# The up-projection of the ConvGatedMLP as a timed plan for four engines

## The chip, the cores and the metric

The kernel runs on one core of a Trainium2 chip. Five engines with queues of their own work side by side: TensorE (PE; its weight loads are PEld), VectorE (DVE), ScalarE (ACT), GpSimd (POOL) and SyncE (SP), which here issues the DMAs. Each engine works through its own instructions strictly in order and waits on semaphores for the others. The metric is the device time of one execution in microseconds (us), as the median of the runs shown.

## The reference

One decoder layer, sequence 1024, width 1024, all in float32: two gated token mixers, then the gated MLP with a causal convolution over three positions, then a gated per-layer embedding, each followed by a layer norm. The part that matters is the MLP's first half, with D_FF = 2816:

```python
h = causal_dwconv(x @ w_up[i], conv_w[i], conv_b[i])     # w_up: 1024 x 5632, three taps per channel
h_gate, h_val = jnp.split(h, 2, axis=-1)
ffn = (jax.nn.silu(h_gate) * h_val) @ w_down[i]
```

## The kernel before

The stages run one after the other: projections and mixers up to 1296 us, the up-projection from 1296 to 1736 us, the down-projection from there, then the embedding. All products are made from float32 operands split into a high part (`wh`, written by ScalarE, L101) and a low part (`wl` = operand minus high part, L106), so that one product is three matmuls (L155): high by high, high by low, low by high.

The up-projection computes x @ w_up in 22 **column pairs** f. A pair is 128 gate columns (block f) and 128 value columns (block 22 + f) for all 1024 positions. It is done as one step of a seven-product scheme for 2 by 2 blocks: the weights of the pair are four blocks 11, 12 (from the gate columns) and 21, 22 (from the value columns), which lie in two raw tiles of 512 KB (`wr` for even f, `ar` for odd f). Four **combinations** are formed in place in these tiles (L164 on VectorE, `wr<-wr,wr` or `ar<-ar,ar`): 11 - 21, 21 + 22, 22 - 11, 12 - 22. Seven operands, numbered j = 0 to 6, are split from the blocks before and after them. A combination overwrites what an earlier low part still reads, so it waits for that low part.

The steps of a pair, with the names used below:

- **products** p0 to p6: twelve matmuls each (4 slices of depth, 3 matmuls), `ch<-xs,wh` and `ch<-xs,wl`, into PSUM banks A to D (`ch`). There are 84 matmuls in a pair. In the order of the program p6 of a pair comes after p1 of the next.
- **sums** (L1043, VectorE, one operand in PSUM): five, which put the two halves of `h` together, and two **copies** on ScalarE (L1050, L1074).
- **convolution** of each half: a start on ScalarE (L1085), two **taps** on VectorE (L1087, both operands in SBUF), and for the gate half a **Silu** on ScalarE (L1089). The value half ("conv1") comes first, the gate half ("conv0") after p6.
- **gating product**: gate times value on GpSimd (L164, `cv<-cv,cv`, 128 x 1024), and its store to `d_act` by SP (L1097).

All seven low parts of a pair from the second on are made by GpSimd. Each operand has one pair of buffers, so the high part j of the next pair waits until product j of this one is done.

Inside this stage the order on each engine is set by the Tile scheduler, which takes the program's order (`up(f)` builds the steps, the loop at the end of the stage runs them) as priority and places every instruction by its own simulation of the engines. The program runs the steps of a pair as

```python
run([p0, p1, *late[:1], p5, *late[1:], p2, p3, p4, conv1])   # late = p6 and conv0 of the pair before
```

with the whole preparation of the pair's weights (`w_sets(f)`) ahead of it, and the gating product within `conv0`.

Of the kernel before, what the change touches and what calls it, by code (L numbers as in the profile page):

```python
# [17 lines left out]
P = 128  # L18
L = 1024
D = 1024  # L20
# [8 lines left out]
NF = FF // P  # L29
# [11 lines left out]
def hybrid_block(ctx: ExitStack, tc: tile.TileContext, x, p, w_in, w_gate_up, b_gate, g_gla, w_gla,  # L41
                 g_ckv, w_uv, w_dsa, w_out, ln1_g, ln1_b, w_up, conv_w, conv_b, w_down, ln2_g, ln2_b,
                 w_ple, w_ple_gate, ln3_g, ln3_b, out, tap=None):
    nc = tc.nc
    V, S, G, T = nc.vector, nc.scalar, nc.gpsimd, nc.tensor
    tap = tap or (lambda name, ap: None)
    x, p, out = x[0], p[0, 0], out[0]
# [13 lines left out]
    wq = pool("wparts", stack=sega)  # L61
# [8 lines left out]
    cw = cp.tile([P, 3, 2 * NF], F32, name="cw")  # L70
    cbias = cp.tile([P, 2 * NF], F32, name="cbias")
# [143 lines left out]
    def quad(a):  # L215
        return a.rearrange("p (a b) -> p a b", b=P)
# [39 lines left out]
    def run(steps):  # L256
        for f in steps:
            f()
# [16 lines left out]
    d_act = [dp.tile([P, 6, L], F32, name=f"d_act{c}") for c in range(4)]  # L275
# [47 lines left out]
    with ExitStack() as mix:  # L323
# [65 lines left out]
        with ExitStack() as c1:  # L389
# [15 lines left out]
            for t in range(NT):  # L405
                ps = bank("sm")
# [13 lines left out]
            for g in range(2):  # L420
                s = slice(g * HALF, (g + 1) * HALF)
# [6 lines left out]
            for j in range(4):  # L428
                un = wload(win_v, 0, KT, [(C_IQ + j * P, C_IQ + (j + 1) * P)], "A", "G")
                for g in range(2):  # L430
                    s = slice(g * HALF, (g + 1) * HALF)
                    ps = bank()
# [3 lines left out]
                                    op=ALU.subtract)  # L436
                    hi = xp.tile([P, HALF], F32R, name=nm("xh"), tag="xh", bufs=2)
# [3 lines left out]
                                    op=ALU.subtract)  # L441
# [3 lines left out]
            for g in range(2):  # L445
                s = slice(g * HALF, (g + 1) * HALF)
# [5 lines left out]
                for k in range(4):  # L452
# [4 lines left out]
                                op=ALU.subtract)  # L457
# [27 lines left out]
            raw = wp.tile([P, 1024], F32, name=nm("wr"), tag="wr", bufs=2)  # L485
# [197 lines left out]
        with ExitStack() as c3:  # L683
# [133 lines left out]
            plan = []  # L817
# [4 lines left out]
            for h in range(DH):  # L822
                b = 4 * h - 2.0 * h / (DH - 1)
# [174 lines left out]
    with ExitStack() as c1:  # L998
        psum_banks(c1, "d", ch=8)
        fp = pool("ffwork", stack=c1)  # L1000
        rawp = pool("raws", stack=segd, side="right")
        wk = pool("upwork", stack=segk, side="right")
        UE, UE0, US = 'GGGGGGG', 'VVGVVGV', 'VVVV'
        nset = [0]

        def blocks(f):

            return (NF + f, f) if f < NF - 1 else (f, NF + f)

        def w_sets(f):  # L1010
# [8 lines left out]
            W = []  # L1019
            for _ in range(7):  # L1020
                n = nset[0] % 7
                nset[0] += 1
                pl, nb = (wq, 4) if n < 4 else (fp, 3)
                W.append([pl.tile([P, 512], F32R, name=nm(x), tag=x, bufs=nb) for x in ("wh", "wl")])
            run(left_operands(raw[1][:, :512], raw[1][:, 512:], raw[0][:, :512], raw[0][:, 512:],
                              lambda j, src: split(*W[j], src, "A", (UE if f else UE0)[j]), US))
            return [[quad(t) for t in w] for w in W]

        def up(f):

            W = w_sets(f)
            st, out_ = {}, {}

            def prod(ps, j, start):
                for k in range(4):
                    mm3(ps, (W[j][0][:, k], W[j][1][:, k]), (XS[j][:, 0, k], XS[j][:, 1, k]), start and k == 0, k == 3,
                        not start)  # L1040

            def plus(out, a, b):
                V.tensor_tensor(out=out, in0=a, in1=quad(b), op=ALU.add)  # L1043

            def p0():
                st["A"] = bank("ch")
                prod(st["A"], 0, True)
                st["h"] = [wk.tile([P, L], F32, name=nm("h"), tag=f"h{i}", bufs=2) for i in range(2)]
                st["hv"] = [h.rearrange("p (a g q) -> p g a q", g=2, q=P) for h in st["h"]]
                S.activation(st["hv"][1][:, 0], quad(st["A"]), AF.Copy)  # L1050

            def p1():
                st["B"] = bank("ch")
                prod(st["B"], 1, True)
                plus(st["hv"][0][:, 1], st["hv"][1][:, 0], st["B"])

            def p5():
                st["C"] = bank("ch")
                prod(st["C"], 5, True)

            def p2():
                st["D"] = bank("ch")
                prod(st["D"], 2, True)

            def p3():
                prod(st["B"], 3, False)
                s1, u3 = st["hv"][1][:, 0], st["hv"][1][:, 1]
                plus(u3, s1, st["B"])
                plus(s1, u3, st["C"])
                plus(u3, u3, st["D"])  # L1070

            def p4():
                prod(st["A"], 4, False)
                S.activation(st["hv"][0][:, 0], quad(st["A"]), AF.Copy)  # L1074

            def p6():
                prod(st["D"], 6, False)
                o = st["hv"][0][:, 1]
                plus(o, o, st["D"])

            def conv(i):
                c = blocks(f)[1 - i]
                h = st["h"][i]
                o = out_[c // NF] = wk.tile([P, L], F32, name=nm("cv"), tag="cv", bufs=3)
                S.activation(o, h, AF.Identity, bias=cbias[:, c:c + 1], scale=cw[:, 2, c:c + 1])  # L1085
                for d in (1, 2):
                    V.scalar_tensor_tensor(o[:, d:], h[:, :L - d], cw[:, 2 - d, c:c + 1], o[:, d:], ALU.mult, ALU.add)  # L1087
                if c < NF:
                    S.activation(o, o, AF.Silu)  # L1089

            def conv1():
                conv(1)

            def conv0():
                conv(0)
                sums(out_[0], out_[0], out_[1], ALU.mult, "G")
                nc.sync.dma_start(d_act[f // 6][:, f % 6], out_[0])  # L1097
            return p0, p1, p5, p2, p3, p4, conv1, p6, conv0
# [18 lines left out]
    with ExitStack() as c1:  # L1117
# [251 lines left out]
```

## Time and profile before

| | us |
|---|---|
| median of 3 runs (2145.47 to 2150.24) | 2145.63 |
| profiled execution: its own time | 2145.27 |
| its span, first to last instruction | 2143.6 |
| TensorE matmul busy | 2063.3 (96%) |
| VectorE busy | 1564.6 (73%) |
| GpSimd busy | 1000.0 (47%) |
| ScalarE busy | 846.0 (39%) |
| mean granted TensorE clock | 0.984 |

The page says that TensorE is busy nearly all the time, but a matmul's busy time is its time in a pipeline, with neighbours overlapping: how fast the matmuls follow one another is read from the timeline, and how long they waited from the rows of a stretch.

### The profile page before, as it was taken

Reading aid. Unit: us, or ns where it says so; the run is one execution under the profiler, and the core shown is the slowest. Engines: PE = TensorE matmul, PEld = TensorE weight load, DVE = VectorE, ACT = ScalarE, POOL = GpSimd, SP = SyncE. Lnnn points to the kernel's source line nnn. Section 1 sums busy time; section 2 is a strip of 40 time slices with the busy share of each in tenths; the row PEclk is TensorE's granted clock in tenths of the full one; section 3 lists DMA queues with packets and bytes.
Section 4 is the critical chain, followed back from the end, with each engine's and each line's share of the span. In section 5 each row is a group of like instructions: output and inputs, shape, how many; then the busy total and the mean of one; then the engine's idle time right before and its main releaser. Section 6 shows DMA issues by size and latency. Waiting matters only on the chain.

```text
span 2143.6 us, 32563 instructions
## 1 busy us (share of the span) xinstructions
PE 2063.3 (96%) x12210; PEld 1811.3 (84%) x12210; DVE 1564.6 (73%) x2742; ACT 846.0 (39%) x1540; POOL 1000.0 (47%) x832
## 2 busy tenths in 40 slices
PE   9999999999999999999999978999999979999997
PEld 8888899998988888887788976877777769989897
DVE  3589999999227888876234487777777788895965
ACT  4343312213126766675222244344344353342421
POOL 2423444535422121213231586776776684554753
PEclk9999999999999999999999998999999989999999
DMA  4322211211226686779766442222222134323222
GB/s 138 79 64 79 86 31 57 57 50 52 64 86 130 130 157 130 144 158 212 205 216 122 147 153 87 86 72 87 81 69 89 64 109 148 118 94 119 89 99 79
DMA packets 377566, 227.14 MB, mean 106 GB/s; under 512 B 189328, under 2 KB 351760, under 8 KB 377408
## 3 DMA queue, kind: packets, MB, share of 16 engines
q1 hardware_dynamic: 377408, 225.06, 38.7%
q8 instruction: 96, 1.57, 0.3%
q14 instruction: 62, 0.51, 0.1%
HBM read 146.37 MB, written 40.89 MB: 87 GB/s over the span
## 4 chain that ended last, share of the span: by engine, by line
PE 29%; DVE 9%; POOL 7%; issue 5%; DMA 3%; ACT 2%; SPq 0%; POOLq 0%; DVEq 0%; ACTq 0%
PE ch L155 16%; PE mm L155 13%; POOL wl L106 4%; DVE cv L1087 1%; DMA wr<-d_ob 1%; DVE cx L164 1%; DMA dr<-in_w_down_dram 1%; DVE h L1043 1%; ACT cv L1085 1%; DVE ar L164 1%; DVE wu L106 1%; DVE res_all L910 1%; DVE res_all L164 0%; DVE stats L933 0%; POOL lnmv L212 0%
## 5 line engine op out<-in xcount | busy, mean ns | idle before, releaser
L106 POOL TENSOR_TENSOR wl<-wr,wh 128x512 fp32r<-128x512 f32 x304 | 439.8, 1461 | 288.3 <-ACT wh L101 280.7
L155 PE MATMUL ch<-xs,wh 128*128 128x512 f32 x1232 | 384.8, 394 | 5.8 <-ACT wh L101 3.2
L155 PE MATMUL mm<-Ah,wh 128*128 128x512 f32 x832 | 332.1, 399 | 2.7 <-ACT wh L101 1.6
L155 PE MATMUL mm<-Al,wh 128*128 128x512 f32 x832 | 330.4, 397 | 0.3 <-POOL Al L106 0.3
L155 PE MATMUL mm<-Ah,wl 128*128 128x512 f32 x832 | 329.4, 396 | 0.0
L155 PEld LDWEIGHTS ch<-xs,wh 128*128 128x128 f32 x1232 | 231.5, 189 | 58.7 <-DVE h L1043 4.1
L103 POOL TENSOR_SCALAR wh<-wr 128x512 fp32r<-128x512 f32 x112 | 75.2, 674 | 381.1 <-PE mm L155 194.4
L155 PE MATMUL ch<-xs,wl 128*128 128x512 f32 x616 | 242.8, 395 | 6.8 <-POOL wl L106 6.7
L155 PE MATMUL mm<-wl,Ah 128*128 128x256 f32 x768 | 217.1, 284 | 5.2 <-POOL wl L106 5.1
L155 PE MATMUL mm<-wh,Al 128*128 128x256 f32 x768 | 215.8, 283 | 0.0
L155 PE MATMUL ch<-wu,au 128*128 128x256 f32 x1512 | 194.0, 292 | 22.5 <-DVE au L106 7.2
L155 PE MATMUL mm<-wh,Ah 128*128 128x256 f32 x768 | 213.2, 283 | 0.0
L1087 DVE SCALAR_TENSOR_TENSOR cv<-h,cw,cv 128x1023 f32<-128x1023 f32 x88 | 168.6, 1915 | 60.0 <-ACT cv L1085 58.5
L155 PEld LDWEIGHTS ch<-wu,au 128*128 128x128 f32 x1512 | 190.4, 199 | 25.9 <-DVE au L106 8.1
L101 ACT ACTIVATE wh<-wr 128x512 fp32r<-128x512 f32 (+1 forms) x201 | 120.5, 623 | 194.7 <-PE mm L155 81.6
L155 PEld LDWEIGHTS mm<-Ah,wh 128*128 128x128 f32 x832 | 156.7, 188 | 33.4 <-ACT wh L101 2.1
L155 PEld LDWEIGHTS mm<-Ah,wl 128*128 128x128 f32 x832 | 156.4, 188 | 33.0
L155 PEld LDWEIGHTS mm<-Al,wh 128*128 128x128 f32 x832 | 156.5, 188 | 30.7 <-POOL Al L106 0.8
L674 DVE MATCH_REPLACE8 score<-m,score 128x896 f32<-128x896 f32 (+3 forms) x192 | 166.5, 869 | 0.0
L673 DVE MAX8 m<-score 128x8 f32<-128x896 f32 (+3 forms) x192 | 163.6, 876 | 2.3 <-POOL score L480 2.1
L155 PEld LDWEIGHTS mm<-wl,Ah 128*128 128x128 f32 x768 | 145.1, 189 | 7.1 <-POOL wl L106 6.4
L155 PEld LDWEIGHTS ch<-xs,wl 128*128 128x128 f32 x616 | 116.5, 189 | 38.2 <-POOL wl L106 14.0
(269 smaller groups left out, 4328.4 us busy)
## 6 DMA issues: line engine op xcount, KB each, us to landing
wr<-in_w_in_dram SPq DMA_DIRECT2D x60, 512.0 KB, 3.8
wr<-in_w_up_dram SPq DMA_DIRECT2D x22, 512.0 KB, 3.9
ar<-in_w_up_dram SPq DMA_DIRECT2D x22, 512.0 KB, 4.0
d_act<-cv SPq DMA_DIRECT2D x22, 512.0 KB, 2.6
dr<-in_w_down_dram SPq DMA_DIRECT2D x12, 768.0 KB, 7.0
ar<-d_act SPq DMA_DIRECT2D x12, 768.0 KB, 5.1
d_tg<-tg SPq DMA_DIRECT2D x32, 256.0 KB, 2.0
wr<-in_w_out_dram SPq DMA_DIRECT2D x16, 512.0 KB, 3.6
```

Source lines behind the costliest of these rows:

```text
L101: S.activation(dst, src, AF.Copy, scale=scale)
L103: (V if eng == "V" else G).tensor_scalar(dst, src, scale, 0.0, ALU.mult, ALU.add)
L106: done["GV"[eng != "G"]] = (G if eng == "G" else V).tensor_tensor(out=dst, in0=src, in1=hi.bitcast(F32), op=ALU.subtract)
L155: T.matmul(ps, lhsT=l, rhs=r, start=start, stop=stop, skip_group_check=more)
L164: (G if eng == "G" else V).tensor_tensor(out=out, in0=a, in1=b, op=op)
L673: V.max(m8, score[t])
L674: V.match_replace(score[t], m8, score[t], TAKEN)
L910: V.scalar_tensor_tensor(r[:, a:b], r[:, a:b], mv[:, 2:3], gb[1][:, a:b], ALU.mult, ALU.add)
L1043: V.tensor_tensor(out=out, in0=a, in1=quad(b), op=ALU.add)
L1085: S.activation(o, h, AF.Identity, bias=cbias[:, c:c + 1], scale=cw[:, 2, c:c + 1])
L1087: V.scalar_tensor_tensor(o[:, d:], h[:, :L - d], cw[:, 2 - d, c:c + 1], o[:, d:], ALU.mult, ALU.add)
```

## The change

`up` and `w_sets` go. In their place stand `plan_weights(f)` and `plan_pair(f)`, which give every operation of a pair a time: t0 = f * PAIR for products, sums, convolutions and store, and t0 = (f - 1) * PAIR for the weights, with PAIR = 7 * ON = 19.04 and ON = 2.72. The operations of all 22 pairs are sorted by this time and issued in that order inside `tc.manual_schedule` for TensorE, VectorE, ScalarE and GpSimd, so that these four keep it; SP is still placed by the scheduler. The times set an order and nothing else: no engine waits for a time. Which engine does an operation, its shape and its operands stay, and the seven low parts stay on GpSimd. The first pair's weights are prepared as before (`first_weights`), and the last pair's gate convolution and store run in the stage behind, as before.

```diff
-        def up(f):
-            W = w_sets(f)
...
-        late = []
         for f in range(NF):
-            p0, p1, p5, p2, p3, p4, conv1, *rest = up(f)
-            run([p0, p1, *late[:1], p5, *late[1:], p2, p3, p4, conv1])
-            late = rest
-        late[0]()
-        last_conv = late[1]
+            if f:
+                plan_weights(f)
+            last_conv = plan_pair(f)
+        with tc.manual_schedule(engines={nc.tensor.engine, nc.vector.engine, nc.scalar.engine, nc.gpsimd.engine}):
+            for _, _, step in sorted(plan, key=lambda e: e[:2]):
+                step()
...
+        def plan_weights(f):
+            t0 = (f - 1) * PAIR
...
+            def hi(t, j, src):
+                def f_():
+                    w[j] = w_place(j)
+                    hi_of(w[j][0], r[src], "A")
+                at_time(t0 + t, f_)
+            def lo(t, j, src):
+                at_time(t0 + t, lambda: lo_of(w[j][1], r[src], w[j][0], "G"))
+            def comb(t, out, x, y, op):
+                at_time(t0 + t, lambda: sums(r[out], r[x], r[y], op))
+            at_time(t0 - 8.0, load)
+            hi(3.3, 0, "11")
+            lo(3.9, 0, "11")
+            comb(6.1, "11", "11", "21", ALU.subtract)
...
+            def store():
+                sums(st["o", 0], st["o", 0], st["o", 1], ALU.mult, "G")
+                sent[0] = nc.sync.dma_start(d_act[f // 6][:, f % 6], st["o", 0])
...
+            last = conv(0, PAIR + 9.0, PAIR + 10.3, PAIR + 13.4) + [(t0 + 2 * PAIR + 5.5, store)]
...
-            last_conv()
+            run(last_conv)
```

What this does to the order shows in the middle of the stage. First GpSimd, from one column pair to the next. In the names `wr` and `ar` tell the pair whose weights are read, and the low parts follow one another as j = 1, 2, 3, 4, then 0 of the next pair. Before:

```order
L164 TENSOR_TENSOR cv_15130<-cv_15130,cv_15034 128x1024
L106 TENSOR_TENSOR wl_15189<-ar_15182,wh_15188 128x512
L106 TENSOR_TENSOR wl_15191<-ar_15182,wh_15190 128x512
L106 TENSOR_TENSOR wl_15193<-ar_15184,wh_15192 128x512
L106 TENSOR_TENSOR wl_15195<-ar_15184,wh_15194 128x512
L106 TENSOR_TENSOR wl_15331<-wr_15328,wh_15330 128x512
L106 TENSOR_TENSOR wl_15199<-ar_15184,wh_15198 128x512
L106 TENSOR_TENSOR wl_15341<-wr_15326,wh_15340 128x512
L164 TENSOR_TENSOR cv_15274<-cv_15274,cv_15178 128x1024
```

And now, with the low parts of j = 5, 1, 2, 3, 4 first:

```order
L106 TENSOR_TENSOR wl_15159<-ar_15017,wh_15158 128x512
L106 TENSOR_TENSOR wl_15182<-ar_15017,wh_15181 128x512
L106 TENSOR_TENSOR wl_15186<-ar_15017,wh_15185 128x512
L106 TENSOR_TENSOR wl_15203<-ar_15019,wh_15202 128x512
L106 TENSOR_TENSOR wl_15225<-ar_15019,wh_15224 128x512
L106 TENSOR_TENSOR wl_15246<-wr_15163,wh_15245 128x512
L164 TENSOR_TENSOR cv_15142<-cv_15142,cv_15064 128x1024
L106 TENSOR_TENSOR wl_15283<-ar_15019,wh_15282 128x512
L106 TENSOR_TENSOR wl_15303<-wr_15161,wh_15302 128x512
```

The gating product (L164) stood between the low parts of j = 5 and j = 1 and took the gate half whose Silu had just been made; now it stands between j = 0 of the next pair and j = 6, and belongs to a pair one earlier.

Second VectorE, over the same stretch: the last combination of a pair's weights, the first two of the next pair's, the sums (lines 1043 and 1111), the gate half's taps (lines 1087 and 1123) and the third combination. Before:

```order
L164 TENSOR_TENSOR ar_15184<-ar_15184,ar_15182 128x512
L164 TENSOR_TENSOR wr_15328<-wr_15328,wr_15326 128x512
L164 TENSOR_TENSOR wr_15326<-wr_15326 128x512
L1043 TENSOR_TENSOR h_15231<-h_15232,ch_15234 128x4x128
L1043 TENSOR_TENSOR h_15087<-h_15087,ch_15137 128x4x128
L1087 SCALAR_TENSOR_TENSOR cv_15274<-h_15087,cw,cv_15274 128x1023
L1087 SCALAR_TENSOR_TENSOR cv_15274<-h_15087,cw,cv_15274 128x1022
L164 TENSOR_TENSOR wr_15326<-wr_15326,wr_15328 128x512
```

And now:

```order
L164 TENSOR_TENSOR ar_15019<-ar_15019,ar_15017 128x512
L1111 TENSOR_TENSOR h_15262<-h_15243,ch_15230 128x4x128
L164 TENSOR_TENSOR wr_15163<-wr_15163,wr_15161 128x512
L164 TENSOR_TENSOR wr_15161<-wr_15161 128x512
L1111 TENSOR_TENSOR h_15118<-h_15118,ch_15145 128x4x128
L1123 SCALAR_TENSOR_TENSOR cv_15286<-h_15118,cw,cv_15286 128x1023
L1123 SCALAR_TENSOR_TENSOR cv_15286<-h_15118,cw,cv_15286 128x1022
L164 TENSOR_TENSOR wr_15161<-wr_15161,wr_15163 128x512
```

Only the sum behind p1 moved: it stands behind the first combination instead of behind the third.

Third TensorE, at the start of a pair, from the end of p0 (`xs_11727`) on; p1 reads `xs_11728`, p5 `xs_12438`, p6 of the pair before `xs_12439`. Before:

```order
L155 MATMUL ch_15362<-xs_11727,wh_15330 128x512 x2
L155 MATMUL ch_15362<-xs_11727,wl_15331 128x512
L155 MATMUL ch_15378<-xs_11728,wh_15332 128x512 x2
L155 MATMUL ch_15405<-xs_12438,wh_15340 128x512 x2
L155 MATMUL ch_15405<-xs_12438,wl_15341 128x512
L155 MATMUL ch_15405<-xs_12438,wh_15340 128x512
L155 MATMUL ch_15281<-xs_12439,wh_15198 128x512
L155 MATMUL ch_15378<-xs_11728,wl_15333 128x512
L155 MATMUL ch_15378<-xs_11728,wh_15332 128x512 x2
```

And now:

```order
L155 MATMUL ch_15354<-xs_11727,wh_15245 128x512 x2
L155 MATMUL ch_15354<-xs_11727,wl_15246 128x512
L155 MATMUL ch_15374<-xs_11728,wh_15325 128x512 x2
L155 MATMUL ch_15374<-xs_11728,wl_15326 128x512
L155 MATMUL ch_15374<-xs_11728,wh_15325 128x512 x2
L155 MATMUL ch_15374<-xs_11728,wl_15326 128x512
```

Before, six matmuls of p5 and p6 stood between the first two matmuls of p1 and the first that reads the low part of j = 1; now this one follows the first two directly, and p6 and p5 come after p1, each in one piece. On ScalarE the order within a pair is nearly the same; the start of the gate half's convolution stands ahead of the high part of j = 5, and the Silu ahead of that of j = 1, in both.

## Rows read from the trace of the kernel before

**Rows 1.** Busy time by stretch: stretch, length, engines (instructions), clock, DMA.

```profile
1322.50:1398.70 76.20, 76.20 (x338) 63.08 (x337) 57.06 (x52) 32.65 (x47) 51.44 (x29) 1.00 0.25 76
1398.70:1736.40 337.70, 330.90 (x1429) 265.29 (x1427) 245.55 (x220) 139.86 (x205) 237.59 (x136) 1.00 0.25 81
```

**Rows 2.** TensorE timeline: start, length, engine, line, operation, names, [idle before, releaser].

```profile
1559.52 0.50 PE L155 MATMUL ch<-xs,wl 128*128 128x512 f32 x1 [0.38 <-POOL wl L106]
...
1571.13 0.61 PE L155 MATMUL ch<-xs,wh 128*128 128x512 f32 x2
```

**Rows 3.** Waits 1296 to 1736: who waited for whom, us in total, times, longest.

```profile
PEld ch L155 <- POOL wl L106: 14.0, 17, 1.1
```

**Rows 4.** GpSimd timeline over one column pair.

```profile
1555.82 2.40 POOL L164 TENSOR_TENSOR cv<-cv,cv 128x1024 f32<-128x1024 f32 x1 [2.37 <-issue]
1558.19 6.99 POOL L106 TENSOR_TENSOR wl<-ar,wh 128x512 fp32r<-128x512 f32 x4
1565.14 1.28 POOL L106 TENSOR_TENSOR wl<-wr,wh 128x512 fp32r<-128x512 f32 x1
1567.78 1.67 POOL L106 TENSOR_TENSOR wl<-ar,wh 128x512 fp32r<-128x512 f32 x1 [1.35 <-ACT wh L101]
1571.52 1.82 POOL L106 TENSOR_TENSOR wl<-wr,wh 128x512 fp32r<-128x512 f32 x1 [2.06 <-ACT wh L101]
1575.70 2.42 POOL L164 TENSOR_TENSOR cv<-cv,cv 128x1024 f32<-128x1024 f32 x1 [2.37 <-issue]
```

**Rows 5.** VectorE timeline over the same column pair.

```profile
1558.49 4.29 DVE L1087 SCALAR_TENSOR_TENSOR cv<-h,cw,cv 128x1023 f32<-128x1023 f32 x2 [1.32 <-ACT cv L1085]
1565.21 1.76 DVE L164 TENSOR_TENSOR ar<-ar,ar 128x512 f32<-128x512 f32 x1 [2.43 <-POOL wl L106]
1566.90 0.68 DVE L164 TENSOR_TENSOR wr<-wr,wr 128x512 f32<-128x512 f32 x1
1567.61 0.69 DVE L164 TENSOR_TENSOR wr<-wr 128x512 f32<-128x512 f32 x1
1568.22 1.28 DVE L1043 TENSOR_TENSOR h<-h,ch 128x512 f32<-128x512 f32 x2
1570.90 3.52 DVE L1087 SCALAR_TENSOR_TENSOR cv<-h,cw,cv 128x1023 f32<-128x1023 f32 x2 [1.40 <-ACT cv L1085]
1574.34 0.68 DVE L164 TENSOR_TENSOR wr<-wr,wr 128x512 f32<-128x512 f32 x1
1574.94 2.12 DVE L1043 TENSOR_TENSOR h<-h,ch 128x512 f32<-128x512 f32 x3
```

**Rows 6.** ScalarE timeline, second half of the same pair.

```profile
1569.62 1.24 ACT L1085 ACTIVATE cv<-h,cbias,cw 128x1024 f32<-128x1024 f32 x1 [1.92 <-DVE h L1043]
1570.77 0.61 ACT L101 ACTIVATE wh<-wr 128x512 fp32r<-128x512 f32 x1
1574.51 1.06 ACT L1089 ACTIVATE cv<-cv 128x1024 f32<-128x1024 f32 x1 [3.12 <-DVE cv L1087]
1575.47 1.66 ACT L101 ACTIVATE wh<-wr 128x512 fp32r<-128x512 f32 x3
1577.09 1.25 ACT L1085 ACTIVATE cv<-h,cbias,cw 128x1024 f32<-128x1024 f32 x1
```

**Rows 7.** GpSimd timeline after the up-projection: its last gating product.

```profile
1767.08 2.70 POOL L164 TENSOR_TENSOR cv<-cv,cv 128x1024 f32<-128x1024 f32 x1
```

**Rows 8.** VectorE timeline beside that gating product.

```profile
1767.92 0.54 DVE L164 TENSOR_TENSOR ar<-ar,cx 128x384 f32<-128x384 f32 x1
...
1768.85 1.35 DVE L164 TENSOR_TENSOR dr<-dr 128x384 f32<-128x384 f32 x1
1770.12 0.55 DVE L164 TENSOR_TENSOR cx<-dr,cx 128x384 f32<-128x384 f32 x1
```

**Rows 9.** TensorE timeline at the start of the up-projection.

```profile
1304.27 2.69 PE L155 MATMUL ch<-xs,wh 128*128 128x512 f32 x5 [3.17 <-ACT wh L101]
```

**Rows 10.** Page, DMA issues: line, queue, count, KB each, us to landing.

```profile
wr<-in_w_up_dram SPq DMA_DIRECT2D x22, 512.0 KB, 3.9
```

More of the change, by code (lines that the diff above doesn't have):

```diff
@@ L1018, in w_sets @@
                 nc.sync.dma_start(raw[-1].rearrange("p (k c) -> p k c", k=KT), wup_v[:, :, c * P:(c + 1) * P])
[L1019 to L1026, printed above, removed]
@@ L1027, in w_sets @@
-            return [[quad(t) for t in w] for w in W]
-        def up(f):
-            W = w_sets(f)
[L1035 to L1081, printed above, removed]
@@ new lines, in raw_weights, with w_place, at_time, first_weights @@
+            return raw[1][:, :512], raw[1][:, 512:], raw[0][:, :512], raw[0][:, 512:]
+        def w_place(j):
+            pl, nb = (wq, 4) if j < 4 else (fp, 3)
+            return [pl.tile([P, 512], F32R, name=nm(x), tag=x, bufs=nb) for x in ("wh", "wl")]
+        plan = []
+        def at_time(t, f):
+            plan.append((t, len(plan), f))
+        W, ST, sent = {}, {}, [None]
+        def first_weights():
+            w = W[0] = {}
+            def put(j, src):
+                w[j] = w_place(j)
+                split(*w[j], src, "A", UE0[j])
+            run(left_operands(*raw_weights(0), put, US))
@@ new lines, in plan_weights, with load @@
+        def plan_weights(f):
+            w, r = {}, {}
+            t0 = (f - 1) * PAIR
+            W[f] = w
+            def load():
+                r.update(zip(("11", "12", "21", "22"), raw_weights(f)))
+            def hi(t, j, src):
+                def f_():
+                    w[j] = w_place(j)
+                    hi_of(w[j][0], r[src], "A")
[8 more added lines that the diff above has]
+            comb(6.1, "11", "11", "21", ALU.subtract)
+            comb(7.0, "21", "21", "22", ALU.add)
+            hi(11.0, 5, "22")
+            lo(11.6, 5, "22")
+            comb(13.3, "22", "22", "11", ALU.subtract)
+            hi(14.4, 1, "22")
+            lo(15.0, 1, "22")
+            hi(15.1, 2, "21")
+            lo(16.1, 2, "21")
+            hi(16.5, 3, "11")
+            lo(17.6, 3, "11")
+            hi(PAIR + 0.9, 4, "12")
+            lo(PAIR + 1.2, 4, "12")
+            comb(PAIR + 3.9, "12", "12", "22", ALU.subtract)
+            hi(PAIR + 8.3, 6, "12")
+            lo(PAIR + 8.9, 6, "12")
@@ new lines, in plan_pair, with prod, f_, half @@
+        def plan_pair(f):
+            t0 = f * PAIR
+            st = ST[f] = {}
+            def prod(n, ps, j):
+                def f_():
+                    start = ps not in st
+                    if start:
+                        st[ps] = bank("ch")
+                    wh, wl = (quad(t) for t in W[f][j])
+                    for k in range(4):
+                        mm3(st[ps], (wh[:, k], wl[:, k]), (XS[j][:, 0, k], XS[j][:, 1, k]), start and k == 0, k == 3,
+                            not start)
+                at_time(t0 + n * ON, f_)
+            def half(i):
+                if ("h", i) not in st:
+                    st["h", i] = wk.tile([P, L], F32, name=nm("h"), tag=f"h{i}", bufs=2)
+                return st["h", i]
+            def part(i, g):
+                return half(i).rearrange("p (a g q) -> p g a q", g=2, q=P)[:, g]
+            def copy(t, i, g, ps):
+                at_time(t0 + t, lambda: S.activation(part(i, g), quad(st[ps]), AF.Copy))
+            def plus(t, out, x, ps):
+                at_time(t0 + t, lambda: V.tensor_tensor(out=part(*out), in0=part(*x), in1=quad(st[ps]), op=ALU.add))
+            def conv(i, ta, tv, ts):
@@ L1082, in conv, with begin @@
                 c = blocks(f)[1 - i]
-                h = st["h"][i]
-                o = out_[c // NF] = wk.tile([P, L], F32, name=nm("cv"), tag="cv", bufs=3)
-                S.activation(o, h, AF.Identity, bias=cbias[:, c:c + 1], scale=cw[:, 2, c:c + 1])
+                def begin():
+                    o = st["o", c // NF] = wk.tile([P, L], F32, name=nm("cv"), tag="cv", bufs=3)
+                    S.activation(o, half(i), AF.Identity, bias=cbias[:, c:c + 1], scale=cw[:, 2, c:c + 1])
+                steps = [(ta, begin)]
@@ new lines, in conv @@
+                    steps.append((tv + 1.5 * (d - 1), tap_))
+                if c < NF:
+                    steps.append((ts, lambda: S.activation(st["o", 0], st["o", 0], AF.Silu)))
+                return [(t0 + t, s) for t, s in steps]
+            def store():
+                sums(st["o", 0], st["o", 0], st["o", 1], ALU.mult, "G")
+                sent[0] = nc.sync.dma_start(d_act[f // 6][:, f % 6], st["o", 0])
+            prod(0, "A", 0)
+            copy(2.8, 1, 0, "A")
+            prod(1, "B", 1)
@@ new lines, in plan_pair @@
+            plus(5.45, (0, 1), (1, 0), "B")
+            prod(3, "C", 5)
+            prod(4, "D", 2)
+            prod(5, "B", 3)
+            plus(16.3, (1, 1), (1, 0), "B")
+            plus(16.9, (1, 0), (1, 1), "C")
+            plus(17.5, (1, 1), (1, 1), "D")
+            prod(6, "A", 4)
+            copy(PAIR + 0.1, 0, 0, "A")
+            prod(9, "D", 6)
+            plus(PAIR + 8.2, (0, 1), (0, 1), "D")
+            last = conv(0, PAIR + 9.0, PAIR + 10.3, PAIR + 13.4) + [(t0 + 2 * PAIR + 5.5, store)]
@@ new lines, in plan_pair @@
+            for t, s in conv(1, 18.7, PAIR + 0.95, PAIR + 4.1) + (last if f < NF - 1 else []):
+                at_time(t, s)
+            return [s for _, s in last]
+        first_weights()
+        for f in range(NF):
+            if f:
[4 more added lines that the diff above has]
+                step()
```

20 lines of the change are left out of this document (8 added, 12 removed).

## The prediction

> **What bounds the kernel now.** I first read the busy times by stretch to see how fast TensorE goes, then its timeline and waits for what it lacks, then the other engines' timelines of one column pair for what makes them late. At full pace three matmuls take 0.68 us (1571.13 to 1571.82 is the step from one such group to the next; the rows of it stand every 0.68 us, of which [rows 2] shows one), so a pair's 84 matmuls take 84 x 0.2267 = 19.04 us. The stretch from 1322.5 to 1398.7 holds four pairs' worth of matmuls and lasts 76.2 = 4 x 19.05 us: full pace. The stretch from 1398.7 to 1736.4 holds 17 pairs' worth and lasts 337.7 us, where 17 x 19.04 = 323.7 would do [rows 1]. So **14.0 us** are lost, 0.83 a pair, at a granted clock of 1.00 in both. The loss is one kind of wait, for a low part from GpSimd: 14.0 us in 17 times [rows 3], one of which stands in [rows 2].
>
> Why is GpSimd late? One pair, from one gating product at 1555.82 to the next at 1575.70, is a closed loop of 19.88 us [rows 4 to 6]. After the product come four low parts (from 1558.19) and a fifth (to 1566.42). Then the combination 12 - 22 on VectorE (ends 1566.97), two more and two sums (to 1569.50), the convolution's start on ScalarE (1569.62 to 1570.86), two taps (1570.90 to 1574.42), the Silu (1574.51 to 1575.57), and with it the next product. Each step waits for the one ahead. GpSimd's idle 2.37 us ahead of the product are the wait for this Silu.
>
> A second thing to see there: **VectorE and GpSimd keep each other out** when the VectorE instruction has both operands in SBUF. A low part takes 1.28 us when nothing is beside it [rows 4], a combination 0.68 [rows 5]. The combination at 1565.21 took 1.76 us; the low part beside it ended at 1566.42, the combination 0.55 later, as if it had only begun then. From 1558.19 four low parts and two taps run in turn and take 6.99 us, 1.17 each: one after the other, not together. A sum, which has an operand in PSUM, takes 0.64 to 0.71 us whatever GpSimd does [rows 5].
>
> **The change, part by part.** What it takes away: the gating product now belongs to a pair whose Silu was made a whole pair ago, so GpSimd no longer waits for it, and the loop above is cut. If nothing else became late, every pair would run at 19.04 and the change would bring the 14.0 us.
>
> What is late next is the loop through VectorE, in the order that the change prints. I put its steps together from the same rows, with the end of the gate half's second tap as zero (1574.42 in the trace). Third combination 0.60 (1575.02); three sums to 2.64 (1577.06); convolution start to 3.92 (1578.34) [rows 5, 6]. Beside this ScalarE makes the Silu and from 1.05 on three high parts; the low part j = 1 starts at about 1.75, 2 at 2.99, by which time the taps of the value half queue up. Then the low parts 2, 3, 4, 0 and the two taps stand in the same turns as the six in [rows 4] from 1558.19, and take the same 6.99: to 9.98. The combination 12 - 22 follows in 0.55: 10.53. Next VectorE has a sum (to 11.13), but **GpSimd has the gating product**, which has been next in its queue since 9.98: 2.41 us less the 0.12 by which a neighbour's end overlaps, to 12.82. The first combination of the next pair can only follow it: 13.37. Low part 6 has waited since 12.8 and goes first, 1.17: 14.54; the second combination 0.55: 15.09; the sum after p6 0.60: 15.69; convolution start 0.12 + 1.24: 17.05; the two taps with the low part j = 5 between them take 3.52 + 0.04, as at 1570.90: **20.6 us** for a pair. That is 0.7 more than the loop before and 1.57 more than TensorE needs. GpSimd is idle from 14.54 until the high part j = 5, which ScalarE makes only behind the convolution's start, so the time is not made up there.
>
> The product's hold is the term that decides. It was harmless before, since VectorE then had three sums and a wait for ScalarE. That a 128 x 1024 product keeps a VectorE instruction out for all of its time shows at the product that runs behind this stage: it ends at 1769.78 [rows 7], an instruction with both operands in SBUF that started beside it at 1768.85 ends at 1770.20, 0.42 after it, and took 1.35 us, while neighbours with an operand in PSUM took 0.54 and 0.55 [rows 8].
>
> The Trainium skill, in SBUF — State Buffer, section "SBUF: two separate sides", says that VectorE (with two SBUF inputs) and GpSimd share one port pair under an exclusive lock, held for the whole instruction by whichever starts first. That speaks against this change, and [rows 7, 8] agree. If the two shared the port at half speed each instead, the first combination would take 2 x 0.68 beside the product and the second as much beside low part 6, and the loop would be about 1.2 us shorter: 19.4, and about 2138 us in all.
>
> How many pairs lose 1.57? The first two pairs have no gating product yet. The plan's own times put the low part j = 1 some 5 us ahead of p1; as p1 has lost the six foreign matmuls that stood ahead of its first low part (6 x 0.2267 = 1.4 us of cover), I count on 3 to 6 us of lead, which is gone after 2 to 4 pairs. So 14 to 17 pairs lose it in full; I take 15.5: 24.3 us.
>
> The start: the row at 1304.27 holds five matmuls in 2.69 us, 0.54 each, of which three now no longer stand ahead of the wait for the first pair's low part j = 1 [rows 9]. Between 0 and 3 x 0.54 = 1.6 us, since that low part may be there by then; I take 0.5. The SP queue: the store moves a pair later, yet in SP's order it still stands right ahead of a load that waits for low part 6 of a later time in the loop (14.54) than the product's end (12.82), so it holds no load back; a load lands in 3.9 us [rows 10], and its first use is over 10 us off. The end: the work of the last pair has the same order on all engines, and the down-projection's order is unchanged: nothing.
>
> Sum, against the profiled execution: 2145.27 - 14.0 + 24.3 + 0.5 = 2156.1. That execution is 0.36 under the median, so about **2156 us**.
>
> **The rivals.** *The plan's pace holds.* If VectorE reaches its combinations before GpSimd's product and low part 6 stand ready, as the plan's own times have it, the loop loses the waits of 1.64 and 1.0 us and is 18.0, under 19.04: 2145.27 - 14.0 + 0.5, about 2132. For it: TensorE did run at 19.04 for four pairs while a lead was there. Against it: the taps alone, at 3.5 to 4.3 us a pair of taps, are longer than the plan's 3.0, so VectorE falls behind within a pair, and once behind, each turn puts it behind GpSimd's queue. It decides by whether VectorE's loop stays under 19.04.
>
> *The first combination slips in ahead of the product.* After low part 4 the combination 12 - 22 and low part 0 want the port within 0.1 us. Should the combination win, the product and the next combination are as close again, and a second win brings the loop to 19.4: 15.5 x 0.36 = 5.6 lost, about 2138. Against it: at 1565.21 the low part won.
>
> *The two loops are alike.* Every hand-over in my sum has 0.1 us of doubt; at 19.9 a pair, 15.5 x 0.86 = 13.3, the change moves the wait and not the time: about 2145.
>
> **How the numbers follow.** Forecast 0.66, within it 20.3 x 14 pairs (2150) to 20.9 x 17 pairs (2164); plan's pace 0.16; combination ahead 0.09; alike 0.09. About 0.3%, 6.4 us, is what a measurement here can tell from no change, so the borders are 2139.2 and 2152.1. Faster: 0.16 and most of the 0.09, 0.22 in all. Same: the alike case, the rest of the combination case and the forecast's low tail of 0.08, 0.20. Slower 0.58. The range leaves out the plan's pace and the far ends: 2137 to 2164; the forecast's own is 2150 to 2164.
>
> **What would show it.** Right: the gating product with no idle time ahead of it on GpSimd; combinations of 1.5 us and more beside it or waiting behind it; pair after pair at 20.3 to 20.9 from about the sixth on, with waits for the low part j = 1 of 1.3 to 1.9 us each. Wrong: 84 matmuls in 19.04 us to the end of the stage, and VectorE idle in wait for products (`ch`) ahead of its sums. If the pace is 19.04 early and gets lost only late, my lead was too small; if the product runs and VectorE's combinations beside it stay at 0.68, my hold is wrong.

## The result and the profile after

| | before | after |
|---|---|---|
| median, us | 2146.07 (2145.47 to 2150.24, 4 runs) | 2158.74 (2156.67 to 2159.23, 4 runs) |
| profiled execution, us | 2145.27 | 2156.67 |
| its span, us | 2143.6 | 2155.0 |

The ratio of after to before is 1.0054, with a 95% interval of 1.004 to 1.0069: the change makes the kernel slower, by 0.5%. 2156 was forecast. Of the run with two halves below, one of four executions took 7193.02 us, and the median given is that of the other three.

First the stretches, in the columns of [rows 1]:

```profile
1322.50:1398.70 76.20, 76.20 (x337) 62.86 (x335) 61.20 (x50) 31.39 (x45) 48.13 (x28) 1.00 0.24 76
1398.70:1747.70 349.00, 333.50 (x1429) 265.54 (x1428) 278.54 (x222) 141.32 (x207) 246.78 (x136) 1.00 0.24 77
```

The first four column pairs behind the first run at TensorE's full pace, as before. The next 17 take 349.0 us where they took 337.7: 11.3 us more, and 25.3 over the 323.7 of full pace. Who waited for whom in the up-projection, in the columns of [rows 3], shows the one wait of before as two:

```profile
PEld ch L155 <- POOL wl L106: 18.1, 17, 1.1
PEld ch L155 <- ACT wh L101: 16.7, 18, 4.7
```

They are at the start of p1, TensorE's timeline says, in every pair from 1398.75 us on (the long one of 4.7 is the stage's start):

```profile
1563.17 0.73 PE L155 MATMUL ch<-xs,wh 128*128 128x512 f32 x2 [0.30 <-ACT wh L101]
1564.54 0.50 PE L155 MATMUL ch<-xs,wl 128*128 128x512 f32 x1 [0.63 <-POOL wl L106]
...
1583.72 0.73 PE L155 MATMUL ch<-xs,wh 128*128 128x512 f32 x2 [0.33 <-ACT wh L101]
```

From one p1 to the next it is 20.55 us, 1.51 over 19.04. TensorE waits for the high part j = 1, makes two matmuls, and waits for the low part. From the fifth pair behind the first on, each pair takes 20.54 to 20.56, counted so.

What makes this pace is seen on the other engines, over the same pair. GpSimd (the product is L164; around it low parts 1 to 4, then 0, and behind it 6 and 5):

```profile
1563.19 7.00 POOL L106 TENSOR_TENSOR wl<-ar,wh 128x512 fp32r<-128x512 f32 x4 [2.83 <-ACT wh L101]
1570.16 1.28 POOL L106 TENSOR_TENSOR wl<-wr,wh 128x512 fp32r<-128x512 f32 x1
1571.40 2.85 POOL L164 TENSOR_TENSOR cv<-cv,cv 128x1024 f32<-128x1024 f32 x1
1574.21 1.74 POOL L106 TENSOR_TENSOR wl<-ar,wh 128x512 fp32r<-128x512 f32 x1
1579.11 1.81 POOL L106 TENSOR_TENSOR wl<-wr,wh 128x512 fp32r<-128x512 f32 x1 [3.16 <-issue]
```

VectorE:

```profile
1557.93 3.51 DVE L1123 SCALAR_TENSOR_TENSOR cv<-h,cw,cv 128x1023 f32<-128x1023 f32 x2 [1.40 <-ACT cv L1118]
1561.37 0.68 DVE L164 TENSOR_TENSOR ar<-ar,ar 128x512 f32<-128x512 f32 x1
1561.97 2.12 DVE L1111 TENSOR_TENSOR h<-h,ch 128x512 f32<-128x512 f32 x3
1565.40 3.64 DVE L1123 SCALAR_TENSOR_TENSOR cv<-h,cw,cv 128x1023 f32<-128x1023 f32 x2 [1.31 <-ACT cv L1118]
1570.23 1.76 DVE L164 TENSOR_TENSOR ar<-ar,ar 128x512 f32<-128x512 f32 x1 [1.19 <-POOL wl L106]
1571.91 0.67 DVE L1111 TENSOR_TENSOR h<-h,ch 128x512 f32<-128x512 f32 x1
1572.51 2.29 DVE L164 TENSOR_TENSOR wr<-wr,wr 128x512 f32<-128x512 f32 x1
1574.83 1.67 DVE L164 TENSOR_TENSOR wr<-wr 128x512 f32<-128x512 f32 x1
1576.42 0.67 DVE L1111 TENSOR_TENSOR h<-h,ch 128x512 f32<-128x512 f32 x1
1578.49 3.51 DVE L1123 SCALAR_TENSOR_TENSOR cv<-h,cw,cv 128x1023 f32<-128x1023 f32 x2 [1.39 <-ACT cv L1118]
```

ScalarE, the two starts of a convolution and the high part j = 5:

```profile
1564.13 1.24 ACT L1118 ACTIVATE cv<-h,cbias,cw 128x1024 f32<-128x1024 f32 x1
...
1577.21 1.24 ACT L1118 ACTIVATE cv<-h,cbias,cw 128x1024 f32<-128x1024 f32 x1 [4.50 <-DVE h L1111]
1578.36 0.62 ACT L101 ACTIVATE wh<-wr 128x512 fp32r<-128x512 f32 x1
```

The product no longer waits: it follows the low part j = 0 at once, where 2.37 us of idle time stood ahead of it in [rows 4]. But the first combination of the next pair (1572.51) takes 2.29 us instead of the 0.68 of [rows 5]: it ends at 1574.80, 0.55 behind the product's end at 1574.25. The second combination (1574.83) takes 1.67 and ends 0.55 behind low part 6. Two waits of 1.61 and 0.98 us a pair are the price of the product's new place. GpSimd then has nothing to do for 3.16 us, until the high part j = 5 comes behind the convolution's start.

### The profile page after: what moved, and what is told of

Read it like the earlier page. It is cut to its first block, busy times and chain, and to the rows that moved or that the text cites. A ratio compares the mean times of both kernels' runs of the same rounds, so it can differ in the third digit from the quotient of the medians.

```text
span 2155.0 us, 32539 instructions
## 1 busy us (share of the span) xinstructions
PE 2066.4 (96%) x12210; PEld 1815.0 (84%) x12210; DVE 1599.7 (74%) x2742; ACT 846.1 (39%) x1540; POOL 1006.2 (47%) x832
## 3 DMA queue, kind: packets, MB, share of 16 engines
q8 instruction: 96, 1.57, 0.3%
## 4 chain that ended last, share of the span: by engine, by line
PE 20%; DVE 14%; ACT 7%; POOL 5%; issue 4%; DMA 3%; SPq 0%; DVEq 0%; POOLq 0%; ACTq 0%
PE mm L155 13%; PE ch L155 6%; DVE cv L1123 4%; POOL wl L106 3%; ACT wh L101 3%; ACT cv L1118 2%; DVE ar L164 2%; DVE wr L164 2%; DVE h L1111 1%; ACT h L1108 1%; DVE cx L164 1%; DMA wr<-d_ob 1%; DMA dr<-in_w_down_dram 1%; DVE wu L106 1%; ACT cv L1127 1%
## 5 line engine op out<-in xcount | busy, mean ns | idle before, releaser
L155 PEld LDWEIGHTS ch<-wu,au 128*128 128x128 f32 x1512 | 190.7, 200 | 24.2 <-DVE au L106 8.3
L1123 DVE SCALAR_TENSOR_TENSOR cv<-h,cw,cv 128x1023 f32<-128x1023 f32 x88 | 155.3, 1765 | 60.0 <-ACT cv L1118 58.4
L106 POOL TENSOR_TENSOR wl<-ar,wh 128x512 fp32r<-128x512 f32 x77 | 128.4, 1684 | 72.1 <-ACT wh L101 40.6
L155 PEld LDWEIGHTS ch<-xs,wl 128*128 128x128 f32 x616 | 116.4, 189 | 42.3 <-POOL wl L106 18.1
```

The lines of the kernel that those rows point to most:

```text
L155: T.matmul(ps, lhsT=l, rhs=r, start=start, stop=stop, skip_group_check=more)
L1123: V.scalar_tensor_tensor(o[:, d:], half(i)[:, :L - d], cw[:, 2 - d, c:c + 1], o[:, d:], ALU.mult, ALU.add)
```

## The experiments

Each is the changed kernel with the edit shown. "A pair" is the time from the first matmul of p1 in one pair to that in the next. The intervals are those of the ratio to the kernel before.

### What the product's hold is worth

```diff
             def store():
-                sums(st["o", 0], st["o", 0], st["o", 1], ALU.mult, "G")
                 sent[0] = nc.sync.dma_start(d_act[f // 6][:, f % 6], st["o", 0])
```

> The changed kernel with the gating product left out (the store sends the gate half alone, so this work is missing from the output). Hold theory (the product on GpSimd keeps VectorE's first combination out, which puts the second behind low part 6): with no product the first combination follows the sum at once, the loop falls under 19.04, all 21 column pairs run at 19.04 and the profiled time falls by 16 x 1.51 + 1 = 25, to about 2131. Rival A (TensorE's new order of products, or ScalarE's, is what is late): the pairs stay at 20.5 and the time at 2155 to 2159. Rival B (the low parts and taps alone fill the shared port): 19.5 to 20, 2140 to 2149.

2131.87 us, ratio 0.993 (0.9915 to 0.9945). Without the product all 21 pairs run at 19.04, to the end of the stage; the stretch's row shows TensorE busy throughout:

```profile
1322.50:1722.10 399.60, 399.60 (x1765) 330.86 (x1763) 289.23 (x271) 179.83 (x251) 189.21 (x143) 1.00 0.26 83
```

So neither TensorE's new order nor the low parts and taps alone are late. What is left open is how the product costs it: by its time on GpSimd, or by keeping VectorE out.

The next run lengthens GpSimd's work at this place, by a second instruction.

```diff
                 sums(st["o", 0], st["o", 0], st["o", 1], ALU.mult, "G")
+                sums(st["o", 0][:, :512], st["o", 0][:, :512], st["o", 1][:, :512], ALU.mult, "G")
```

> The changed kernel with half a product more (128 x 512, once more on the same tile, so the output has the value half applied twice there); GpSimd works some 1.2 us longer at the same place of each pair. Hold theory: each us of the product is a us of the loop, so 20.55 becomes 21.7 to 21.8, from about the third or fourth pair on, and the time rises by 17 to 19 x 1.2 and the lead lost earlier: 2177 to 2181. Rival (GpSimd stands idle for 6 us a pair and takes it in there): 20.55 stays, 2157 to 2160.

2163.73 us (1.0064 to 1.0094), and a pair takes 20.55 as in the kernel after: the forecast of 21.7 was wrong, and the rival's 20.55 held, though its range for the time did not. Where the pair's time would have to show, GpSimd has 4.55 us of products instead of 2.85:

```profile
1571.32 4.55 POOL L164 TENSOR_TENSOR cv<-cv,cv 128x1024 f32<-128x1024 f32 x2
1575.84 1.74 POOL L106 TENSOR_TENSOR wl<-ar,wh 128x512 fp32r<-128x512 f32 x1
```

and VectorE beside it

```profile
1572.43 2.29 DVE L164 TENSOR_TENSOR wr<-wr,wr 128x512 f32<-128x512 f32 x1
1574.76 1.66 DVE L164 TENSOR_TENSOR wr<-wr 128x512 f32<-128x512 f32 x1
```

shows the very two waits of the kernel after. The first combination comes in between the long product and the added one; the second comes behind the added one, which stands where low part 6 stood, and low part 6 falls into the 3.16 us in which GpSimd had nothing to do. My expectation counted microseconds of GpSimd's work, but in these rows VectorE waits for **instructions**, one at each of its own. It also means that GpSimd's total is not what is late. The 5 us over the kernel after don't come from these pairs: TensorE leaves them at 1747.6, after's time, and in the down-projection it has a wait that after doesn't have,

```profile
PE ch L155 <- DVE res_all L1227: 4.1, 1, 4.1
```

The trace leads it back to the last pair. Its added instruction stands three low parts behind its product on GpSimd,

```profile
1785.91 1.30 POOL L164 TENSOR_TENSOR cv<-cv,cv 128x512 f32<-128x512 f32 x1
```

so its store goes out at 1787.24, in the kernel after at 1781.30. The loads of `res_all` come behind that store in SP's queue, at 1790.01 instead of 1784.07, and VectorE's step on `res_all`, for which TensorE waits, waits for them. No run tests this chain.

The test of the reading that VectorE waits for instructions is to divide the same product.

```diff
-                sums(st["o", 0], st["o", 0], st["o", 1], ALU.mult, "G")
+                for c in range(0, L, 512):
+                    sums(st["o", 0][:, c:c + 512], st["o", 0][:, c:c + 512], st["o", 1][:, c:c + 512], ALU.mult, "G")
```

> The changed kernel with the gating product issued as two instructions of 128 x 512 in the same place; the work is the same. Hand-over theory (an instruction of GpSimd holds the port to its own end, and then a waiting instruction of VectorE comes next): the first combination follows the first half, the second combination the second half, and low part 6 comes after both, beside a sum: 1.2 us less, 19.35 a pair. That is only 0.3 over TensorE's 19.04, so the lead of the first pairs lasts for most of the stage: 2131 to 2138. Rival (what counts is GpSimd's total work, or the place of the product in its queue): 20.55 stays, 2156 to 2160.

2137.58 us, ratio 0.9952 (0.9935 to 0.9969). The first nine pairs behind the first run at 19.04, and from the eleventh on a pair takes 19.45 to 19.49: 1.09 less than 20.55, near the 1.2 expected, and the time is in the range. GpSimd's line of both halves:

```profile
1640.69 3.44 POOL L164 TENSOR_TENSOR cv<-cv,cv 128x512 f32<-128x512 f32 x2
```

and the two combinations, of which the first now waits only for one half:

```profile
1641.80 1.18 DVE L164 TENSOR_TENSOR wr<-wr,wr 128x512 f32<-128x512 f32 x1
1643.01 1.67 DVE L164 TENSOR_TENSOR wr<-wr 128x512 f32<-128x512 f32 x1
```

The same with steps of 256:

```diff
-                sums(st["o", 0], st["o", 0], st["o", 1], ALU.mult, "G")
+                for c in range(0, L, 256):
+                    sums(st["o", 0][:, c:c + 256], st["o", 0][:, c:c + 256], st["o", 1][:, c:c + 256], ALU.mult, "G")
```

> The changed kernel with the gating product issued as four instructions of 128 x 256. Hand-over theory: the first combination waits for one quarter and the second for the next; the third and fourth quarter and low part 6 run beside the sum behind p6 and the convolution's start; 18.7 a pair, under 19.04: full pace to the end of the stage, 2130 to 2134. Rival: 20.55 and a little more for the three instructions added, 2157 to 2162.

2133.51 us, ratio 0.9936 (0.9922 to 0.9951), full pace to the end:

```profile
1323.20:1723.00 399.80, 399.80 (x1766) 330.91 (x1764) 307.62 (x271) 175.73 (x251) 306.56 (x227) 1.00 0.26 83
```

GpSimd does the quarters in 4.24 us, since VectorE's instructions come in between them; the two combinations take 0.68 and 1.11. So the first one waits for no quarter, where I had expected one: the first quarter ran beside the sum behind p1. Only the second waits for one.

```profile
1650.32 4.24 POOL L164 TENSOR_TENSOR cv<-cv,cv 128x256 f32<-128x256 f32 x4
```

```profile
1651.43 0.68 DVE L164 TENSOR_TENSOR ar<-ar,ar 128x512 f32<-128x512 f32 x1
1652.14 1.11 DVE L164 TENSOR_TENSOR ar<-ar 128x512 f32<-128x512 f32 x1
```

The same work on the same engine at the same place, in four pieces instead of one, makes 25 us of difference to the kernel after. The 18.7 a pair that I expected can't be seen, since TensorE's 19.04 sets the pace.

Third, the product on VectorE itself.

```diff
-                sums(st["o", 0], st["o", 0], st["o", 1], ALU.mult, "G")
+                sums(st["o", 0], st["o", 0], st["o", 1], ALU.mult)
```

> The changed kernel with the gating product on VectorE at the same time of the plan (between the combination 12 - 22 and the first one). The port is held some 1.1 us for it where GpSimd needed 2.4. Hold theory: the first combination comes some 1.3 us earlier, the loop is under 19.3 and the time 2131 to 2137. Rival (VectorE, whose busy time a pair rises from 16.5 to 17.6 us, is what is late): 20.5 or more, 2156 to 2165.

2152.55 us (1.001 to 1.0033); a pair takes 20.19 from the sixth on. Both expectations missed. The product does take half the time, 1.21 us:

```profile
1647.30 0.68 DVE L1111 TENSOR_TENSOR h<-h,ch 128x512 f32<-128x512 f32 x1
1647.90 1.21 DVE L164 TENSOR_TENSOR cv<-cv,cv 128x1024 f32<-128x1024 f32 x1
1649.04 1.77 DVE L164 TENSOR_TENSOR wr<-wr,wr 128x512 f32<-128x512 f32 x1
1650.85 0.69 DVE L164 TENSOR_TENSOR wr<-wr 128x512 f32<-128x512 f32 x1
```

but while VectorE makes it, the high part j = 6 is done and low part 6 comes up on GpSimd, whose line is

```profile
1648.18 2.08 POOL L106 TENSOR_TENSOR wl<-ar,wh 128x512 fp32r<-128x512 f32 x1 [1.35 <-ACT wh L101]
```

It is waiting when the product ends and goes next; the first combination waits for it, 1.77, and only the second is undisturbed. From the end of the sum to the end of the second combination it is 3.56 us (1647.98 to 1651.54), in the kernel after 3.92 (1572.58 to 1576.50): 0.36 less, just the difference between 20.55 and 20.19. What I left out is who comes next on the port: the product went out of the way, and low part 6 took its turn.

### What the product's old place is worth

```diff
-            last = conv(...) + [(t0 + 2 * PAIR + 5.5, store)]
+            last = conv(...) + [(t0 + PAIR + 14.6, store)]
```

> The changed kernel with the product alone put back to its own pair, right behind its Silu (between the low parts 5 and 1, as before the change). If the product's new place is the whole of the loss: the loop of before, 19.9, about 2145 to 2147. Hold theory worked out with the one other thing that moved on VectorE (the sum behind p1 now stands ahead of the first combination): the first combination ends 0.6 later than in the kernel before, low part 6 gets the port ahead of the second one (1.2), the loop is 19.9 + 0.85 to 1.0 = 20.7 to 20.9 and the time 2157 to 2163: the product's return gains nothing until that sum moves too. Rival A (TensorE's order): 20.5, 2157.

2163.54 us, ratio 1.0082 (1.0067 to 1.0097); a pair takes 20.83, as expected, and the time is 0.5 us over the range. The product's return alone makes it worse than the kernel after. VectorE's lines show why. The sum behind p1 (1555.42) stands ahead of the combination 11 - 21, the first of the next pair, as in the kernel after; before the change it stood behind the second, 21 + 22. (Where the section on the change counts "the first combination" and "the third" for this sum, it counts along its list, which begins with 12 - 22.)

```profile
1553.73 1.76 DVE L164 TENSOR_TENSOR wr<-wr,wr 128x512 f32<-128x512 f32 x1 [2.43 <-POOL wl L106]
1555.42 0.67 DVE L1111 TENSOR_TENSOR h<-h,ch 128x512 f32<-128x512 f32 x1
1556.02 0.68 DVE L164 TENSOR_TENSOR ar<-ar,ar 128x512 f32<-128x512 f32 x1
1556.73 1.66 DVE L164 TENSOR_TENSOR ar<-ar 128x512 f32<-128x512 f32 x1
```

Low part 6 comes up on GpSimd beside the first combination,

```profile
1556.30 1.54 POOL L106 TENSOR_TENSOR wl<-wr,wh 128x512 fp32r<-128x512 f32 x1 [1.35 <-ACT wh L101]
```

and the second (1556.73) takes 1.66 behind it; in [rows 5] both took 0.68 and 0.69, since no sum stood ahead of them. So the next run puts that sum back too:

```diff
-            plus(5.45, (0, 1), (1, 0), "B")
+            plus(7.6, (0, 1), (1, 0), "B")
```

> As the run with the product in its own pair, and the sum behind p1 moved behind the second combination, so that all that uses the shared port stands in the order of the kernel before, and TensorE keeps the new order (whole products). Hold theory: 19.9 a pair from about the sixth on, 2145 to 2147, the kernel before within its noise; TensorE's whole products are worth nothing. Rival A (TensorE's new order costs by itself, since the low part j = 1 has 1.4 us less cover): 20.3 to 20.8, 2152 or more.

2144.08 us, ratio 0.999 (0.9981 to 1.0); a pair takes 19.84 to 19.94 from the fifth on, the pace of the kernel before, and the time is 0.9 us under the range. TensorE waits about as often as before, though for a little longer in all; first this run, then the kernel before:

```profile
PE ch L155 <- POOL wl L106: 9.0, 17, 0.6
```

```profile
PE ch L155 <- POOL wl L106: 6.7, 16, 0.6
```

So the change's whole effect on this stage sits in the place of two operations, the product and one sum. TensorE's whole products, the biggest visible part of the new order, are worth nothing that can be measured here. The product in its new place with the sum in its old one was not run, so what the sum adds in the changed kernel is not shown.

The control for the four quarters is to divide the product here, where VectorE has sums beside it:

```diff
-            plus(5.45, (0, 1), (1, 0), "B")
+            plus(7.6, (0, 1), (1, 0), "B")
...
-            last = conv(...) + [(t0 + 2 * PAIR + 5.5, store)]
+            last = conv(...) + [(t0 + PAIR + 14.6, store)]
...
-                sums(st["o", 0], st["o", 0], st["o", 1], ALU.mult, "G")
+                for c in range(0, L, 256):
+                    sums(st["o", 0][:, c:c + 256], st["o", 0][:, c:c + 256], st["o", 1][:, c:c + 256], ALU.mult, "G")
```

> The order of the kernel before on the shared port, and the product as four instructions of 128 x 256: the control for the four quarters. Hand-over theory: here VectorE has one combination and then three sums beside the product, so it waits for it little, and dividing it gains nothing: 19.85 to 19.95 a pair, 2142 to 2147. Rival (four short instructions are worth their gain wherever they stand): 19.5 or less, 2139 or less.

2154.99 us, ratio 1.0043 (1.0027 to 1.006); a pair takes 20.29 to 20.37, 0.45 more than undivided. The reading "the gain isn't general" holds, but my number was wrong: the product in four takes 2.85 us where [rows 4] has 2.40 and 2.42 for one,

```profile
1642.73 2.85 POOL L164 TENSOR_TENSOR cv<-cv,cv 128x256 f32<-128x256 f32 x4 [2.36 <-issue]
```

and in this order the product is itself a step of the loop (Silu, product, low part 1), so the 0.43 of dividing is paid in every pair.

### What else is in the loop

Low part 5 runs between the taps of the gate half, because its high part stands behind the convolution's start on ScalarE.

```diff
-            hi(11.0, 5, "22")
+            hi(8.9, 5, "22")
```

> The changed kernel with one time altered: the high part j = 5 stands ahead of the start of the gate half's convolution on ScalarE. The product and its hold stay. Loop theory (20.55 is a sum of steps, one of which is low part 5 between the two taps, because its high part comes only after the convolution's start): low part 5 runs while VectorE sums and waits for ScalarE, the loop loses 1.2 us less 0.1 to 0.2, 19.4 to 19.5, and the lead of the first pairs lasts to the second half of the stage: 2132 to 2140. Rival (the hold alone sets the pace): 20.55 stays, 2156 to 2160.

2143.08 us, ratio 0.9985 (0.9976 to 0.9995). Five pairs behind the first at 19.04, and from the seventh on 19.61 to 19.70: 0.9 less than 20.55. GpSimd now makes low parts 6 and 5 one behind the other,

```profile
1643.50 1.73 POOL L106 TENSOR_TENSOR wl<-ar,wh 128x512 fp32r<-128x512 f32 x1
1645.19 1.74 POOL L106 TENSOR_TENSOR wl<-wr,wh 128x512 fp32r<-128x512 f32 x1
```

and the taps

```profile
1647.77 2.60 DVE L1123 SCALAR_TENSOR_TENSOR cv<-h,cw,cv 128x1023 f32<-128x1023 f32 x2 [1.39 <-ACT cv L1118]
```

take 2.60 instead of 3.51. That is the gain, 0.91, where I had taken a whole low part, 1.2 less 0.1 to 0.2. The rest goes back because two taps alone take 1.30 each, more than the 1.17 that each instruction took where taps and low parts ran in turn ([rows 4]).

So the loop ends above the 19.4 to 19.5 expected, the lead is gone by the seventh pair, and the time is 3 us over the range.

The same on top of the old places of product and sum:

```diff
-            hi(11.0, 5, "22")
+            hi(8.9, 5, "22")
...
-            plus(5.45, (0, 1), (1, 0), "B")
+            plus(7.6, (0, 1), (1, 0), "B")
...
-            last = conv(...) + [(t0 + 2 * PAIR + 5.5, store)]
+            last = conv(...) + [(t0 + PAIR + 14.6, store)]
```

> The order of the kernel before on the shared port (product in its own pair, sum behind p1 late), and the high part j = 5 ahead of the gate half's convolution start. Loop theory: low part 5 between the taps cost 0.91 where it was taken out (3.51 to 2.60 for the two taps); 19.87 - 0.91 = 18.96, just under 19.04: full pace to the end of the stage, 2131 to 2136, so the new place of the product isn't needed for it. Rival (GpSimd's wait for the Silu sets the pace of this order, whatever low part 5 does): 19.87 stays, 2142 to 2146.

2130.53 us, ratio 0.9927 (0.9912 to 0.9942), the best of all, and 0.5 under the range. The estimate 19.87 - 0.91 = 18.96 is just under TensorE's 19.04; the loop's own length can't be seen, but full pace to the end agrees with it:

```profile
1321.40:1721.30 399.90, 399.90 (x1766) 331.12 (x1764) 281.60 (x271) 177.35 (x251) 276.46 (x164) 1.00 0.26 83
```

This kernel has the plan's code with three times in it altered: the product at PAIR + 14.6, the sum at 7.6, the high part j = 5 at 8.9. It is 28 us faster than the changed kernel and 16 faster than the one before. That the runs at full pace (2130.5, 2131.9, 2133.5) differ by 3 us is not from the up-projection's pairs: in the profiled executions of the fastest and the slowest of the three, 1.75 us of it lies ahead of p1 of the second pair (1321.40 and 1323.15) and 1.4 behind the stage. What causes either is open.

## Why the prediction was right

**The loop.** The sum of steps in the prediction can be laid beside the rows of after, with the end of the gate half's second tap (1557.93 + 3.51 = 1561.44) as zero:

| step | predicted | measured |
|---|---|---|
| third combination ends | 0.60 | 0.61 |
| low part 1 starts | 1.75 | 1.75 |
| three sums end | 2.64 | 2.65 |
| low part 0 ends | 9.98 | 10.00 |
| combination 12 - 22 ends | 10.53 | 10.55 |
| product ends | 12.82 | 12.81 |
| first combination ends | 13.37 | 13.36 |
| low part 6 ends | 14.54 | 14.51 |
| second combination ends | 15.09 | 15.06 |
| convolution start ends | 17.05 | 17.01 |
| second tap ends | 20.6 | 20.56 |

No step is off by more than 0.04. Every duration was a row of before, every order was printed, and waits between the two engines had been read as whole instructions, from [rows 4, 5, 7, 8].

**The sum.** Predicted: 15.5 pairs by 1.57, 24.3, against 14.0 before. Measured: 16 pairs by 1.51, 24.2, and 1.1 more, nearly all in the last pair, 25.3 in all against 14.0. The lead of 2 to 4 pairs was just under four. The 0.5 at the start did not show in the time: p1 of the second pair starts at 1322.43, before at 1322.52. Counted from the stage's first matmul (1295.08, before 1295.61) it comes 0.4 later, but this stretch takes 26.9 to 28.3 us over the runs of the plan, so the rows don't settle this term. That the sum meets the profiled execution to 0.6 us (2156.1 and 2156.67) is in part luck, since 1.0 too little for the pairs and 0.5 too much for the start cancel in part. The end of the stage to the end of the kernel takes 407.3 us, before 407.1: nothing, as predicted. So the stage explains 11.3 of the 11.4 by which the profiled executions differ. The median lies 2.07 above the profiled execution, where the forecast had added the 0.36 of before; so the forecast is nearly 3 us under the median.

**The signs.** The product without idle time ahead of it and combinations of 1.5 us and more were right. "Pair after pair at 20.3 to 20.9" was right too, from the fifth on. "Waits for the low part j = 1 of 1.3 to 1.9 us each" was wrong in its form: the 1.51 comes as a wait for the high part and one for the low part, which is 1.1 us by the rows of the weight loads (18.1 in 17 times), since TensorE reaches p1 before either.

**The rivals.** The plan's pace, 2132, falls for this order, but not as an idea: it was put down to VectorE's loop staying under 19.04, and the runs that bring it there (four quarters, high part 5 early with the product in its old place) do come out at 2130 to 2134. The first combination ahead of the product did not occur: the pairs at 20.55 repeat within 0.02, and the combination beside the product takes 2.28 or 2.29 us in 17 pairs in a row. Two loops alike, 2145, falls with the time. Sharing the port at half speed, 19.4 a pair and about 2138, falls too. Here the Trainium skill, SBUF — State Buffer, section "SBUF: two separate sides", has an exclusive lock for the whole instruction instead. The rows agree: the first combination ends 0.55 us behind the product, and in the run with two halves the first combination's wait falls from 1.61 to 0.50 us with the instruction's size alone.

**What was wrong** in the mechanism stands in the expectations: I took a microsecond of the product for a microsecond of the loop (the long product: none), the product on VectorE for a gain of 1.3 (0.36), the dividing for free (0.43 a pair where the product is a step of the loop).

## What to carry to other kernels

When VectorE and GpSimd both work from SBUF, cost an operation on GpSimd by the VectorE instruction that will come up beside it, and not by GpSimd's busy time: write down which instructions queue for the port in turn, with the durations of the old trace and the new order, and add up the loop. A wait that is removed from GpSimd can be worth less than nothing if its time had kept the engine out of VectorE's way. Long instructions off the critical path can be divided where someone waits behind them, and should stay whole where they are a step themselves.

## What the runs showed of the hardware

- VectorE (with both operands in SBUF) and GpSimd pass the port to each other by turns. In the rows shown here, when an instruction of one engine ended and one of the other was waiting for it, the waiting one came next, even with more queued on the first: the combination between the long product and the added one (2.29 us, as without the added one), and between two halves (1.18). So in these rows an instruction waits for one instruction of the other engine, however many stand in its queue.
- Dividing a GpSimd product of 128 x 1024 into four costs 0.43 us beside VectorE's sums (2.85 against 2.42), 0.14 for each instruction added.
- The same product takes 1.21 us on VectorE and 2.42 on GpSimd.
